# Last feed-forward block: three output tiles preset with x2 in DRAM, their scaled rows from ScalarE added by accumulating transfers

## The chip, the cores and the metric

The kernel runs on one core of a Trainium2 chip. Its time is the device time of one execution in microseconds (us); given is the median of several runs. Beside it stands one execution under the hardware profiler, whose records the pages of this document quote. The engines are TensorE (PE in the profile), VectorE (DVE), ScalarE (ACT), GpSimd (POOL) and SyncE (SP, which only issues transfers).

## What is computed

One layer of a hybrid encoder for a prompt of 2048 rows and 8 x 16 = 128 sample rows, all in float32, 1024 columns wide:

```python
h   = rms_norm(x, g[0]);  z = h @ w_in
att = rms_norm(band_attention(z), g_att);  mem = mlstm(z)
x2  = x + rms_norm(concat(att, mem) @ w_out, g[1])
u   = rms_norm(x2, g[2]) @ w_up             # 2 x 2816 columns
y   = causal_conv3(u) + b_conv
ffn = (gelu(y_gate) * y_up) @ w_down        # 2816 -> 1024
out = x2 + rms_norm(ffn, g[3])              # the output
```

What matters here is the last line: each row of `ffn` is multiplied by `g[3]` and by one factor, 1 / sqrt(mean of its squares + eps), and added to the row of `x2`.

## The kernel before

The 2176 rows are 17 tiles of 128 rows: tiles 0 to 15 are the prompt, tile 16 (`SAMPLE`) the sample rows. After attention and memory, a projection phase writes `x2` tile by tile to DRAM, each tile of 512 KB as its own tensor `x2d[t]` (line 1045). The feed-forward part then runs over three blocks of tiles (`FBLOCKS`); the last one has tiles 12, 13, 14, 15 and SAMPLE, numbered j = 0 to 4.

Each float32 matmul is done as three matmuls on split operands (`mm3`, lines 105 to 107): a high part made by a cast on ScalarE (line 1327, `wdh` for weights, `ah` for activations) and a low part, the difference, made on VectorE (line 1328, `wdl` and `al`). So each load passes through ScalarE, then VectorE, then TensorE. The split buffers rotate: `wdh` and `wdl` have two each, `ah` and `al` share four, and a cast into one waits until TensorE has done with its former contents.

The down projection uses seven products of half blocks (Strassen's scheme, `SEQUENCE`), numbered p = 0 to 6. Each product has three stretches of weights (c = 0 to 2), loaded by `down_rows` (line 1382) from `w_down` or from sums kept in DRAM (`wtd`), and six pieces of activations, loaded by `fetch_a` (lines 1573 and 1576) and split by `split_a`. After each product of the last block, `leave_last` moves or adds the sums from PSUM to the tiles `F_[j]` in SBUF (named `last` in the profile). When half a row (512 columns) is complete, `seal` closes it: ScalarE squares it and sums the squares (line 1705 or 1709), VectorE multiplies it by `g3` (line 1706 or 1708). When both halves are there, GpSimd makes the factor `rs` from the sums (lines 88 and 94), VectorE computes `F * rs + x2` (line 1717) and SP stores the result (line 1718). For j = 0, 1 and 4 this happens after p = 5, while TensorE runs the product p = 6; for j = 2 and 3 after p = 6, at the very end.

The `x2` rows for that sum are loaded at line 1738 into `X_[j]`, tiles that reuse the buffers of the up projection's operands. Tiles of the earlier blocks are finished another way (`later`, lines 1443 to 1452): their scaled rows are added to `x2d` in DRAM by accumulating transfers that GpSimd issues (line 1449), and copied to the output from there (line 1451).

The code is laid out by a framework that orders the instructions of each engine itself, by the order of the code and by when it estimates them ready, and sets all the semaphores. So the order on an engine, and on SP's queue of transfers, need not be that of the code.

Of the kernel before, what the change touches and what calls it, by code (L numbers as in the profile page):

```python
# [12 lines left out]
AF = mybir.ActivationFunctionType  # L13
ALU = mybir.AluOpType
# [26 lines left out]
NK = NF // 2  # L41
FOLD_RATE = 1.0
FAST = (0, 1, 2)
ORDERS = [[f for k in range(NK) for f in (k, k + NK)] if b in FAST else list(range(NF)) for b in range(3)]
B11, B12, B22, B21 = range(4)
T1, T3, T2, T4 = range(4, 8)
# [4 lines left out]
def hymba_step(ctx: ExitStack, tc: tile.TileContext, I: dict, O: dict):  # L51
    nc = tc.nc
# [20 lines left out]
    def dt_(shape, name):  # L73
        return dram.tile(shape, F32, tag=name, name=name)
# [12 lines left out]
    def mean_square(ms, ssq, n, eps=EPS):  # L87
        nc.gpsimd.tensor_scalar(ms, ssq, 1.0 / n, eps, op0=ALU.mult, op1=ALU.add)

    def rsqrt_mean(ssq, n, name, eps=EPS):  # L90
        ms = small.tile([P, 1], F32, tag="ms", name=name + "_ms")
        mean_square(ms, ssq, n, eps)
        rs = small.tile([P, 1], F32, tag="rs", name=name + "_rs")
        nc.gpsimd.tensor_tensor(rs, ms, nhalf[:, 0:1], op=ALU.pow)
        return rs
# [7 lines left out]
    def mm3(out, ah, al, bh, bl, start, stop, onto=False):  # L103
# [18 lines left out]
    f1d = [dt_([P, 512], f"f1d{t}") for t in range(12)]  # L122
    gd = {b: [dt_([P, 768], f"gd{b}_{f}") for f in range(NF)] for b in range(3) if b not in FAST}
    ad = {(b, what): dt_([P, NK, 256 if b == 2 and what in ("A22", "S2", "S3") else 384], f"ad{b}_{what}")
          for b in FAST for what in ("A11", "A12", "A22", "S1", "S2", "S3", "S4")}
    wtd = [dt_([P, 2048], f"wtd{k}") for k in range(NK)]
    wsd = [dt_([P, 2048], f"wsd{f}") for f in range(NF)]
    lated = [dt_([P, 4, 384], f"lated{i}") for i in range(4)]
    x2d = [dt_([P, D], f"x2d{t}") for t in range(17)]
# [1229 lines left out]
    def load_up(b, i, g, quads=None):  # L1359
        f = ORDERS[b][i]  # L1360
        n = 2 * i + g
        nm = f"{b}_{f}_{g}"
        if n % 3 < 2:
            h = wpool.tile([P, 2112], F32R, tag="wh", name=f"wuh{nm}", bufs=2)
            l = wpool.tile([P, 2112], F32R, tag="wl", name=f"wul{nm}", bufs=2)
            at = [(h[:, i * 512:(i + 1) * 512], l[:, i * 512:(i + 1) * 512]) for i in range(4)]
        else:
            t = [p4.tile([P, 1056], F32R, tag="w3", name=f"wu3{nm}_{i}", bufs=4) for i in range(4)]
            at = [tuple(t[2 * x + i // 2][:, i % 2 * 512:i % 2 * 512 + 512] for x in range(2)) for i in range(4)]
        for (h, l), r in zip(at, quads or load_quads(b, f, g)):  # L1370
            split(h, l, r)
        return at
# [46 lines left out]
    def out_rows(t):  # L1419
        return O["y_sample"] if t == SAMPLE else O["y_prompt"][t * P:(t + 1) * P, :]  # L1420
# [63 lines left out]
    for b, tiles in enumerate(FBLOCKS):  # L1484
        last = b == len(FBLOCKS) - 1
        fast = b in FAST
        nt = len(tiles)
# [133 lines left out]
        unfinished = []  # L1621
        for fi, f in enumerate(ORDERS[b]):
            w = pend.pop(0)
# [63 lines left out]
        if fast:  # L1687
# [3 lines left out]
            if last:  # L1691
                place = lambda pool, i: pool.tile([P, 3, D], F32, tag=f"B{i}", name=f"last{i}", bufs=1)
                fa, xa, fb, xb = place(p3, 0), place(p3, 1), place(p4, 3), place(p4, 4)
                F_ = [fa[:, 0], fa[:, 1], fb[:, 0], fb[:, 1], fa[:, 2]]
                X_ = [xa[:, 0], xa[:, 1], xb[:, 0], xb[:, 1], xa[:, 2]]

            def part_of(j, dh):
                return F_[j][:, dh * 512:dh * 512 + 512]

            def seal(j, dh, acc=None):  # L1700

                t, half, gs = tiles[j], part_of(j, dh), g3[:, dh * 512:dh * 512 + 512]
                ssq = p3.tile([P, 1], F32, tag=f"dssq{j}", name=f"dssq{t}_{dh}", bufs=2)
                if acc is None:
                    nc.scalar.activation(junk, half, AF.Square, accum_out=ssq)
                    nc.vector.tensor_tensor(half, half, gs, op=ALU.mult)
                else:
                    nc.vector.tensor_tensor(half, acc, gs, op=ALU.mult)
                    nc.scalar.activation(junk, acc, AF.Square, accum_out=ssq)
                if j not in res:  # L1710
                    mean_square(ssq, ssq, D)
                    res[j] = ssq
                    return
                rs = rsqrt_mean(ssq, D, f"n3_{t}", res[j])
                for c in ((slice(0, D),) if acc is None else (slice(512, D), slice(0, 512))):
                    v = F_[j][:, c]
                    nc.vector.scalar_tensor_tensor(v, v, rs, X_[j][:, c], op0=ALU.mult, op1=ALU.add)
                    nc.sync.dma_start(out_rows(t)[:, c], v)

            def leave_last(p):  # L1720
                acc = sets[SEQUENCE[p][2]]
                for j in range(2):
                    if p == 0:
                        nc.scalar.copy(part_of(j, 0), acc[j])
                    elif p == 2:
                        nc.scalar.copy(part_of(j, 1), acc[j])
                    elif p == 3:
                        nc.scalar.copy(part_of(2 + j, 1), acc[j])
                    elif p == 6:
                        seal(2 + j, 0, acc[j])  # L1730
                    else:
                        x = part_of(*{1: (j, 0), 4: (2 + j, 1), 5: (j, 1)}[p])
                        nc.vector.tensor_tensor(x, x, acc[j], op=ALU.add)
                        seal(*{1: (j, 0), 4: (2 + j, 1), 5: (j, 1)}[p])
                if p == 0:
                    nc.scalar.copy(part_of(4, 1), mms[0])
                    for j in range(5):
                        nc.sync.dma_start(X_[j], x2d[tiles[j]])
                elif p == 1:
                    nc.scalar.copy(part_of(4, 0), mms[0])  # L1740
                    seal(4, 0)
                elif p == 5:
                    nc.vector.tensor_tensor(part_of(4, 1), part_of(4, 1), mms[1], op=ALU.add)
                    seal(4, 1)
# [84 lines left out]
        for dh in range(2):  # L1829
# [57 lines left out]
            for j in order:  # L1887
# [5 lines left out]
                else:  # L1893
# [4 lines left out]
                    rs = p3.tile([P, 1], F32, tag=f"drs{j}", name=f"drs{tiles[j]}", bufs=2)  # L1898
# [101 lines left out]
```

## Time and profile before

| | us |
|---|---|
| median of 3 runs | 2754.65 |
| lowest and highest run | 2751.52, 2759.46 |
| profiled execution, time | 2753.91 |
| profiled execution, span of its records | 2752.2 |

| engine | busy us | share of the span |
|---|---|---|
| TensorE | 2677.0 | 97% |
| VectorE | 1922.8 | 70% |
| ScalarE | 1457.1 | 53% |
| GpSimd | 731.5 | 27% |

The page counts TensorE as busy from a matmul's start to its modelled end. The granted clock, which its other views give, is TensorE's share of full speed. The lines of a timeline read: start, length, engine, line of the kernel, operation, output <- inputs, shapes, count, and in brackets how long the engine stood idle before and what released it. In a view by lines, a group has its count, then busy time in all and the mean of one in nanoseconds, then the idle time ahead of it. A "q" behind an engine's name is its queue of issues.

### The profile page before, as it was taken

Reading aid. Unit: us, or ns where it says so; the run is one execution under the profiler, and the core shown is the slowest. Engines: PE = TensorE matmul, PEld = TensorE weight load, DVE = VectorE, ACT = ScalarE, POOL = GpSimd, SP = SyncE. Lnnn points to the kernel's source line nnn. Section 1 sums busy time; section 2 is a strip of 40 time slices with the busy share of each in tenths; the row PEclk is TensorE's granted clock in tenths of the full one; section 3 lists DMA queues with packets and bytes.
Section 4 is the critical chain, followed back from the end, with each engine's and each line's share of the span. In section 5 each row is a group of like instructions: output and inputs, shape, how many; then the busy total and the mean of one; then the engine's idle time right before and its main releaser. Section 6 shows DMA issues by size and latency. Waiting matters only on the chain.

```text
span 2752.2 us, 47852 instructions
## 1 busy us (share of the span) xinstructions
PE 2677.0 (97%) x16323; PEld 2504.0 (91%) x16323; DVE 1922.8 (70%) x3643; ACT 1457.1 (53%) x2961; POOL 731.5 (27%) x1397
## 2 busy tenths in 40 slices
PE   8999999999999999999999999999999999999998
PEld 7899999998899998878999997799999878999976
DVE  5344456646556667766999997758888866998956
ACT  4355545634356666543555456655455665554554
POOL 1000010211100002344465551123343212556401
PEclk9999999999999999999999999999999999999999
DMA  5534355557564456678776668757886867798875
GB/s 185 159 115 141 104 162 169 165 149 213 155 192 131 139 171 223 195 235 279 286 210 197 198 199 286 239 185 209 240 238 184 263 227 233 228 263 233 252 265 178
DMA packets 337172, 557.04 MB, mean 202 GB/s; under 512 B 62083, under 2 KB 168415, under 8 KB 336799
## 3 DMA queue, kind: packets, MB, share of 16 engines
q1 hardware_dynamic: 252846, 400.31, 47.2%
q0 software_dynamic: 45488, 119.84, 14.8%
q10 hardware_dynamic: 38592, 33.83, 3.7%
q8 instruction: 128, 2.10, 0.3%
q14 instruction: 118, 0.96, 0.1%
HBM read 389.77 MB, written 173.49 MB: 205 GB/s over the span
## 4 chain that ended last, share of the span: by engine, by line
PE 43%; DVE 4%; DMA 3%; issue 1%; ACT 1%; POOL 0%; SPq 0%; DVEq 0%; POOLq 0%; ACTq 0%
PE uec L105 5%; PE uec L106 5%; PE uec L107 5%; PE dn L107 3%; PE dn L105 3%; PE dn L106 3%; PE ua L107 3%; PE ua L106 3%; PE ua L105 3%; PE dnm L107 1%; PE dnm L106 1%; PE ub L107 1%; PE dnm L105 1%; PE ub L105 1%; PE ub L106 1%
## 5 line engine op out<-in xcount | busy, mean ns | idle before, releaser
L105 PE MATMUL uec<-B,wuh 128*128 128x384 f32 (+1 forms) x720 | 236.2, 328 | 6.0 <-DVE ug L1501 3.3
L106 PE MATMUL uec<-B,wuh 128*128 128x384 f32 (+1 forms) x720 | 235.3, 327 | 0.0
L107 PE MATMUL uec<-B,wul 128*128 128x384 f32 (+1 forms) x720 | 234.4, 327 | 0.0
L1327 ACT CAST wuh<-wu 128x512 fp32r<-128x512 f32 x255 | 141.7, 618 | 105.9 <-PE uec L106 104.5
L107 PE MATMUL dn<-wdh,al 128*128 128x512 f32 x462 | 186.0, 403 | 4.7 <-DVE al L1328 4.5
L1328 DVE TENSOR_TENSOR al<-ar,ah 128x768 fp32r<-128x768 f32 (+2 forms) x141 | 108.6, 779 | 116.4 <-ACT ah L1327 114.1
L105 PE MATMUL dn<-wdh,ah 128*128 128x512 f32 x462 | 183.8, 398 | 5.9 <-ACT ah L1327 3.7
L106 PE MATMUL dn<-wdl,ah 128*128 128x512 f32 x462 | 182.6, 395 | 0.0
L1327 ACT CAST ah<-ar 128x768 fp32r<-128x768 f32 (+2 forms) x141 | 96.2, 692 | 152.3 <-PE dnm L106 112.9
L1328 DVE TENSOR_TENSOR wul<-wu,wuh 128x512 fp32r<-128x512 f32 x255 | 164.5, 685 | 2.4 <-ACT wuh L1327 2.4
L406 DVE CUSTOM_DVE_ANT_0 tmp<-s,nb 128x640 f32<-128x640 f32 (+4 forms) x128 | 94.4, 738 | 89.9 <-PE s L396 89.3
L105 PE MATMUL vo<-wi_h,hT 128*128 128x256 f32 x544 | 155.2, 285 | 0.6 <-DVE mt L212 0.6
L107 PE MATMUL vo<-wi_h,hT 128*128 128x256 f32 x544 | 155.6, 286 | 0.0
L106 PE MATMUL vo<-wi_l,hT 128*128 128x256 f32 x544 | 154.8, 285 | 0.0
L1328 DVE TENSOR_TENSOR wdl<-wdr,wdh 128x512 fp32r<-128x512 f32 x231 | 145.5, 686 | 8.5 <-ACT wdh L1327 8.3
L105 PEld LDWEIGHTS uec<-B,wuh 128*128 128x128 f32 x720 | 135.2, 188 | 9.2 <-issue 3.7
L106 PEld LDWEIGHTS uec<-B,wuh 128*128 128x128 f32 x720 | 135.4, 188 | 0.2
L107 PEld LDWEIGHTS uec<-B,wul 128*128 128x128 f32 x720 | 135.1, 188 | 0.0
L105 PE MATMUL qk<-hT,wi_h 128*128 128x384 f32 (+1 forms) x384 | 129.0, 336 | 5.9 <-ACT qk_st L237 5.2
L419 DVE TENSOR_TENSOR ptl<-pt,pth 128x640 fp32r<-128x640 f32 (+4 forms) x128 | 93.6, 738 | 57.8 <-ACT pth L418 56.9
L1327 ACT CAST wdh<-wdr 128x512 fp32r<-128x512 f32 x231 | 127.5, 620 | 11.3 <-PE uec L106 7.5
L407 ACT ACTIVATE tmp<-tmp,mn 128x640 f32<-128x640 f32 (+4 forms) x128 | 97.6, 763 | 64.2 <-DVE mn L406 61.8
(426 smaller groups left out, 9258.8 us busy)
## 6 DMA issues: line engine op xcount, KB each, us to landing
wu<-in_w_up SPq DMA_DIRECT2D x220, 256.0 KB, 4.8
wu<-wsd SPq DMA_DIRECT2D x176, 256.0 KB, 3.4
wdr<-wtd SPq DMA_DIRECT2D x132, 256.0 KB, 4.8
wi_raw<-in_w_in SPq DMA_DIRECT2D x52, 512.0 KB, 4.0
wdr<-in_w_down SPq DMA_DIRECT2D x99, 256.0 KB, 4.7
wsd<-ws POOLq DMA_DIRECT2D x88, 256.0 KB, 4.3
ar<-ad_S SPq DMA_DIRECT2D x50, 384.0 KB, 3.4
kraw<-kTd SPq DMA_DIRECT2D x112, 128.0 KB, 3.3
```

The lines of the kernel that those rows point to most:

```text
L105: nc.tensor.matmul(out, ah, bh, start=start, stop=False, skip_group_check=onto)
L106: nc.tensor.matmul(out, ah, bl, start=False, stop=False, skip_group_check=onto)
L107: nc.tensor.matmul(out, al, bh, start=False, stop=stop, skip_group_check=onto)
L406: nc.vector.tensor_tensor_reduce(o_, s_, b_, 1.0, 3e38, ALU.add, ALU.min, accum_out=mn)
L407: nc.scalar.activation(tmp[:, :n], tmp[:, :n], AF.Exp, bias=mn, scale=-1.0, accum_out=rsum[:, i % 4, hh:hh + 1])
L419: nc.vector.tensor_tensor(s.ptl[:, sl, qc], ptv, s.pth[:, sl, qc], op=ALU.subtract)
L1327: nc.scalar.copy(h, r)
L1328: nc.vector.tensor_tensor(l, r, h, op=ALU.subtract)
```

## The change

For j = 0, 1 and 4 of the last block (tiles 12, 13 and SAMPLE, named `SENT`), `x2` is no longer loaded into SBUF: line 1738 copies it, DRAM to DRAM, into the output rows. When the factor `rs` is known, ScalarE multiplies the 1024 columns of `F_[j]` by it, in place, and GpSimd issues one transfer of 512 KB that adds them to the output rows in DRAM. VectorE's line 1717 and SP's line 1718 remain for tiles 14 and 15 alone.

```diff
+SENT = (0, 1, 4)
...
                 rs = rsqrt_mean(ssq, D, f"n3_{t}", res[j])
+                if acc is None and j in SENT:
+                    nc.scalar.activation(F_[j], F_[j], AF.Copy, scale=rs)
+                    nc.gpsimd.dma_start(out_rows(t), F_[j], accum_op=ALU.add)
+                    return
                 for c in ((slice(0, D),) if acc is None else (slice(512, D), slice(0, 512))):
                     v = F_[j][:, c]
                     nc.vector.scalar_tensor_tensor(v, v, rs, X_[j][:, c], op0=ALU.mult, op1=ALU.add)
...
                     for j in range(5):
-                        nc.sync.dma_start(X_[j], x2d[tiles[j]])
+                        nc.sync.dma_start(out_rows(tiles[j]) if j in SENT else X_[j], x2d[tiles[j]])
```

## The prediction

> **What bounds the kernel now.** I read the page first: the span and the share of each engine.
>
> ```profile
> span 2752.2 us, 47852 instructions
> PE 2677.0 (97%) x16323; PEld 2504.0 (91%) x16323; DVE 1922.8 (70%) x3643; ACT 1457.1 (53%) x2961; POOL 731.5 (27%) x1397
> ```
>
> TensorE (PE) is busy for 97% of the span, so work that moves between other engines counts only where TensorE waits for it. The arithmetic that the change touches (line 1717) runs in the last block, so I read next the chain of work that ended last, in order of time, near the end (start, length, what).
>
> ```profile
> 2734.88 0.60 DVE wdl L1328
> 2735.48 1.20 DVE last L1717
> 2736.68 0.60 DVE wdl L1328
> 2737.28 0.61 DVE al L1328
> 2737.94 0.50 PE dn L107
> ```
>
> Here VectorE (DVE) sets the end, and one of the three instructions that the change removes stands in it. TensorE's timeline shows the price; its third line is the last matmul of the kernel.
>
> ```profile
> 2735.78 0.39 PE L106 MATMUL dn<-wdl,ah 128*128 128x512 f32 x1
> 2737.94 0.50 PE L107 MATMUL dn<-wdh,al 128*128 128x512 f32 x1 [1.77 <-DVE al L1328]
> 2743.07 0.40 PE L107 MATMUL dn<-wdh,al 128*128 128x512 f32 x1
> ```
>
> TensorE stood still for 1.77 us, until `al`, the low part of the activations, came from DVE. The busy times by windows show what followed (columns: length, busy time of PE, PEld, DVE, ACT, POOL, granted clock, DMA share, GB/s).
>
> ```profile
> 2735.55:2738.96 3.41, 1.64 (x7) 1.08 (x6) 2.67 (x4) 0.37 (x1) 0.00 (x0) 0.97 0.77 310
> 2738.96:2742.37 3.41, 3.41 (x9) 2.63 (x9) 0.00 (x0) 0.00 (x0) 0.00 (x0) 0.53 0.00 0
> 2739.00:2742.10 3.10, 3.10 (x8) 2.36 (x8) 0.00 (x0) 0.00 (x0) 0.00 (x0) 0.50 0.00 0
> 2620.00:2625.00 5.00, 3.00 (x12) 1.81 (x12) 1.39 (x2) 1.89 (x4) 0.26 (x1) 1.00 1.08 352
> ```
>
> Right behind a stretch of 3.41 us in which PE worked for 1.64 us, the clock was 0.50 for 3.10 us. That costs another 3.10 x 0.5 = 1.55 us, if the pause caused it. The last row warns that it need not: 2.00 us of idle in five left the clock at 1.00.
>
> **What is removed.** Three additions of 1024 columns leave DVE. Its timeline there, then ScalarE's (ACT):
>
> ```profile
> 2731.19 1.29 DVE L1717 SCALAR_TENSOR_TENSOR last<-last,n_rs,last 128x1024 f32<-128x1024 f32 x1
> 2733.61 1.27 DVE L1717 SCALAR_TENSOR_TENSOR last<-last,n_rs,last 128x1024 f32<-128x1024 f32 x1
> 2735.41 1.27 DVE L1717 SCALAR_TENSOR_TENSOR last<-last,n_rs,last 128x1024 f32<-128x1024 f32 x1
> 2737.20 1.02 DVE L1328 TENSOR_TENSOR al<-ar,ah 128x512 fp32r<-128x512 f32 x2
> ...
> 2729.53 0.62 ACT L1327 CAST ah<-ar 128x512 fp32r<-128x512 f32 x1 [0.58 <-PE dn L106]
> 2730.05 1.66 ACT L1327 CAST wdh<-wdr 128x512 fp32r<-128x512 f32 x3
> 2732.51 0.62 ACT L1327 CAST ah<-ar 128x512 fp32r<-128x512 f32 x1 [0.80 <-PE dn L106]
> 2735.52 0.41 ACT L1327 CAST ah<-ar 128x256 fp32r<-128x256 f32 x1 [2.38 <-DVE wdl L1328]
> ```
>
> From 2731.19 DVE worked without a pause, and each addition held its queue for 1.2 us, 3.6 us in all. The late `al` needs only the `ah` that ACT finished at 2732.51 + 0.62 = 2733.13. Without the additions DVE gets to it at 2737.20 - 3.6 = 2733.6 and is done at 2734.2. PE wants it when the matmul of 2735.78 lets it go on, at 2737.94 - 1.77 = 2736.17. So the pause has a slack of about 2 us and goes, if ACT keeps its times. Next late would be the third `wdl`, which moves to about 2733 and is early too; then nothing but PE's own matmuls.
>
> **What ACT gets.** Three scalings of 1024 columns by a per-row factor. No such instruction is in the trace; the nearest:
>
> ```profile
> L229 ACT ACTIVATE hT<-xr 128x1024 fp32r<-128x1024 f32 x17 | 18.0, 1058 | 11.2 <-DMA xr<-in_x_prompt 7.7 <-DMA xr<-in_x_sample 3.3
> L1520 ACT ACTIVATE y<-uu,wcv 128x768 f32<-128x768 f32 x44 | 45.3, 1030 | 52.0 <-DVE uu L1663 52.0
> L1524 ACT ACTIVATE y<-y 128x768 f32<-128x768 f32 x44 | 37.3, 847 | 79.9 <-DVE y L1522 79.9
> ```
>
> 1024 columns take 1.06 us without a factor per row; a factor and an offset per row add 1.03 - 0.85 = 0.18 us. Each scaling lies between 1.06 and 1.24; I take 1.15, so 3.45 us for three. ACT's own gaps before 2735.52 are 0.80 + 2.38 = 3.18 us, and each factor comes from GpSimd (POOL):
>
> ```profile
> 2728.40 0.89 POOL L94 TENSOR_TENSOR n_rs<-n_ms,nhalf 128x1 f32<-128x1 f32 x1
> 2731.49 1.39 POOL L94 TENSOR_TENSOR n_rs<-n_ms,nhalf 128x1 f32<-128x1 f32 x1
> 2745.02 0.27 POOL L88 TENSOR_SCALAR n_ms<-dssq,dssq 128x1 f32<-128x1 f32 x1 [12.13 <-ACT junk L1709]
> ```
>
> The first factor is ready at 2729.3, the third at 2732.9. Behind a waiting scaling on ACT's queue stand the casts that make `wdh` and `ah`, and behind those DVE and PE. If all three scalings go ahead of the `ah` of 2732.51, it ends at 2729.53 + 0.6 + 1.6 + 3.45 + 0.6 = 2735.8, `al` follows at 2736.5, and PE waits 0.3 us beyond the 2736.17. If one goes behind it, nothing waits. I keep 0.3 us.
>
> **The transfers.** Three stores of SP's queue (line 1718) become accumulating transfers issued by POOL. Before, nothing of the remaining weight loads stood behind those stores. On POOL an issue takes 0.89 us (first row below), 2.7 us in all, inside the 12.13 us in which POOL waited; if two issues go ahead of the third factor, that one is 1.8 us later.
>
> ```profile
> L1449 POOL DMA_DIRECT2D x2d<-f x24: 842/894/3290, 1896.2 to 2524.7; - x24
> ...
> DMA to landing us min/median/max: 4.7/6.4/9.0
> ...
> 2746.74 2.86 SPq L1718 DMA_DIRECT2D out_y_prompt<-last  x4
> ```
>
> The existing accumulating transfers of 256 KB land after 4.7 to 9.0 us. For 512 KB I bound the time by 4.7 below and twice 9.0 = 18 above, and take twice 4.7 = 9.4, since the queues are nearly empty there (DMA share 0.00 in the rows from 2739 on). The last scaling ends near 2735.5, its issue at 2736.4, and its data land near 2745.8, ahead of the four last stores, which SP issues from 2746.74 on. So I cost them at nothing; at 18 us the last would land at 2754.4 and would itself be the end. The Trainium skill, "DMA: Bandwidth & Descriptors", section "Anatomy of one DMA — SWDGE (gpsimd) path", gives about 2.0 us plus bytes over 436 GB/s; as an estimate that is 3.2 us here, and the sum would be the same.
>
> **The presets.** Three of the five loads of x2 (line 1738) become copies from x2 to the output, both in DRAM: the same bytes read, the same count of issues, but no buffer to wait for. Where do they go? SP's queue is not in code order, as the second row shows: line 1905, the program's second last transfer, stands among weight loads at 2607. The others show the loads now, and when x2 is stored and lands, and how SP has waited for such landings from 1200 to 1400 us (total, times, longest).
>
> ```profile
> L1738 SPq DMA_DIRECT2D last<-x2d x5: 319/422/524, 2585.8 to 2593.4; - x5
> 2607.17 0.42 SPq L1905 DMA_DIRECT2D out_conv_prompt<-halo  x1
> L1045 SPq DMA_DIRECT2D x2d<-mx x17: 319/326/446, 1072.8 to 1327.1; - x17
> DMA to landing us min/median/max: 2.6/4.7/9.3
> SPq L1018 <- DMA x2d<-mx: 31.2, 8, 9.0
> ...
> 1200.00:1330.00 130.00, 125.81 (x604) 101.98 (x603) 84.03 (x114) 53.98 (x110) 65.66 (x114) 1.00 0.89 301
> 2610.00:2640.00 30.00, 26.73 (x114) 20.79 (x113) 16.48 (x26) 13.65 (x24) 4.50 (x7) 1.00 0.91 315
> ```
>
> A preset may therefore stand anywhere after its x2 has landed, more than a thousand us early. Wherever PE has cover it costs nothing, which is my central value. The bounds: at worst each of the three blocks SP for 4.7 us in front of other loads, 14.1 us, and their 1.57 MB take 5.2 us at the 301 GB/s of that window, whose DMA share is already 0.89: 19.3 us. At best the 1.57 MB that are missing from 2585 to 2593 shorten the 3.27 us that PE idles from 2610 to 2640.
>
> **Sum.** -1.77 (pause) - 1.55 (half clock) + 0.3 (ACT) + 0 (transfers, presets) = -3.0 us. The profiled execution took 2753.91 us, 1.7 more than its span, and would become 2750.9. The median of the runs, 2754.65, is 0.74 above it, so I forecast 2751.6 us. The work after the last matmul, 2752.2 - 2743.5 = 8.7 us, stays. That is 0.11% less, under the 0.3% (8.3 us) which a measurement of this kernel can about tell from no change.
>
> **Rivals.**
> 1. The half clock stays. For it: the idle of 2620 to 2625 left the clock at 1.00, so 1.77 us need not be what lowered it. Against: the row of 1.64 us busy in 3.41 stands just ahead of the half clock. Then only 1.77 - 0.3 = 1.5 us go: 2753.2 us. The Trainium skill, "TensorE: Matmul & The Clock Gate", section "Part 1: The HAM clock gate", speaks for this rival: it has the clock fall after at least one idle window of about 3.4 us, which PE did not have here; the length of the slow stretch agrees with its window.
> 2. Presets early and in the way (slower than before). They stand behind the stores of x2 between about 1200 and 1330 us and hold up SP's loads, with the DMA share at 0.89. It decides once they cost PE more than the 3.0 us gained. For it: SP waited up to 9.0 us for just such landings; against: PE was 97% busy there all the same, so loads have some cover. Half of its bound is 9.6 us: 2761 us, at the bound 2771.
> 3. Faster than the sum: the loads from 2585 on have the queues to themselves, and the 3.27 us after 2610 go as well: 2748.3 us. A changed order of SP's queue could also remove other waits, which I cannot price; against it: those loads were issued by 2593.4, 17 us before that stretch begins.
> 4. ACT or the accumulation late. The third factor waits behind two POOL issues (1.8 us) and its scaling stands ahead of `ah`: the pause returns at 0.3 + 1.8 = 2.1 us, and nothing is gained: 2755 us. Or the last accumulation lands at 2754.4 and the time is 2757.
>
> **How the numbers follow.** The forecast has 0.37, rival 1 0.12, rival 2 0.30, rival 3 0.13 and rival 4 0.08. Faster by over 0.3% (below 2746.4) needs rival 3 and more: 0.12, with a part of the forecast's spread. Slower by over 0.3% (above 2762.9) needs the upper half of rival 2 and some of its neighbours: 0.22. The rest, 0.66, is within. The range leaves out the upper end of rival 2 and the unpriced part of rival 3: 2744 to 2764.
>
> **What would show it.** Right: no line 1717 of 1024 columns on DVE; PE's pause before the last 16 matmuls below 0.5 us; clock 1.00 to the last matmul, near 2740; three ACT scalings of about 1.15 us between 2729 and 2736; accumulations landed by 2746. Wrong: a half clock without a pause; SP waiting for x2 to land at more places from 1200 to 1330 us, with PE idle above 4.2 us there; the chain ending in a POOL transfer.

## The result and the profile after

The changed kernel took 2763.12 us, the median of 11 runs (2758.05 to 2770.87); the kernel before, in the same sitting, 2755.06 us (11 runs, 2751.30 to 2763.36). The ratio is 1.0025, with an interval from 1.0013 to 1.0037: by this ratio the change costs some 7 us, where 3 us less was forecast. A second set of runs of the same kernel gave 1.0018 [1.0006, 1.0029]. Both intervals leave 1.0 out, and both central values lie under the 0.3% called measurable in the prediction. One execution of a kernel further down (presets late) took 3731.02 us at a mean granted clock of 0.655, and ratios leave it out.

The profiled execution of the changed kernel was the longest of its 11 runs (2770.87 us), so its times can't be subtracted from those of before as they stand. I read it stage by stage instead. First the page, then the three scalings by lines (durations in ns: least, median, most), and TensorE's timeline at the end, each of the changed kernel:

```profile
span 2769.2 us, 47845 instructions
PE 2682.8 (97%) x16323; PEld 2508.4 (91%) x16323; DVE 1919.7 (69%) x3640; ACT 1460.2 (53%) x2964; POOL 729.8 (26%) x1400
...
L1717 ACT ACTIVATE last<-last,n_rs x3: 1136/1140/1147, 2751.1 to 2753.2; 128x1024 f32<-128x1024 f32 x3
...
2755.27 0.39 PE L107 MATMUL dn<-wdl,ah 128*128 128x512 f32 x1
2755.66 0.50 PE L108 MATMUL dn<-wdh,al 128*128 128x512 f32 x1
2759.23 0.40 PE L108 MATMUL dn<-wdh,al 128*128 128x512 f32 x1
```

Three instructions went from VectorE to ScalarE (3643 to 3640, 2961 to 2964). Between the `wdl,ah` and the `wdh,al` matmul, where TensorE stood still for 1.77 us before, the second starts at 2755.66, when the first ends. GpSimd's last issue, the busy times by windows with the clock, the transfers there (size, us from issue to landing) and the last issues of SP:

```profile
2754.67 0.85 POOL L1718 DMA_DIRECT2D out_y_sample<-last  x1 [0.17 <-issue]
...
2751.00:2754.40 3.40, 3.40 (x17) 2.77 (x16) 2.21 (x4) 3.40 (x5) 3.00 (x4) 1.00 0.32 19
2754.40:2757.80 3.40, 3.39 (x14) 2.25 (x13) 1.03 (x2) 0.81 (x2) 0.95 (x2) 1.00 0.90 163
2757.80:2761.20 3.40, 1.83 (x8) 1.13 (x7) 0.77 (x2) 0.69 (x2) 0.00 (x1) 1.00 1.03 199
...
out_y_prompt<-last POOLq DMA_DIRECT2D x2, 512.0 KB, 7.0
out_y_sample<-last POOLq DMA_DIRECT2D x1, 512.0 KB, 9.9
...
2762.91 2.94 SPq L1723 DMA_DIRECT2D out_y_prompt<-last  x4
```

The clock is 1.00 to the last matmul. So the end of the kernel went as forecast: from the 16300th matmul to the last one this execution takes 3.12 us less than before. One thing there was not forecast: from the end of the last matmul (2759.23 + 0.40) to the end of the span it takes 9.5 us, where before it was 8.7.

The loss must lie elsewhere. The presets (line 1743 now) went where rival 2 of the prediction had put them, more than a thousand us early:

```profile
L1743 SPq DMA_DIRECT2D out_y_prompt<-x2d x2: 553/559/565, 1304.3 to 1319.5; - x2
L1743 SPq DMA_DIRECT2D out_y_sample<-x2d x1: 737/737/737, 1235.0 to 1235.0; - x1
```

But SP did not wait longer for landings of `x2` because of them. These are the rows of its waits, in the first and the second profile of the changed kernel (us in total, times, longest):

```profile
SPq L1019 <- DMA x2d<-mx: 33.4, 8, 8.6
...
SPq L1019 <- DMA x2d<-mx: 34.9, 8, 8.5
```

Before it was 31.2 us, 8 times, and in a kernel without early copies (presets in the middle, below) 33.4 us, 8 times. What TensorE waited for between 1300 and 1380 us had changed, though. Its waits in the second profile of the changed kernel:

```profile
PE ua L106 <- ACT mt L1035: 1.8, 1, 1.8
PE wo L108 <- DVE mt L213: 0.9, 1, 0.9
PE uec L106 <- ACT wu L1328: 0.9, 1, 0.9
PE ub L108 <- DVE wu L1329: 0.6, 1, 0.6
```

A product of the up projection (`ua`) now waits for ScalarE's reading of the projection phase's last sums (`mt`). That set the question for the runs.

### Which instructions moved

The traces also give the order in which the instructions stand on each engine. Between before and after, 423 of TensorE's 16323 matmuls and some 240 instructions of VectorE stand elsewhere in the order, and about 110 each of ScalarE and GpSimd; SP's queue has the three copies put in and is otherwise the same up to the last block. Apart from the end and from single records, the differences belong to the stretch from about 1320 to 1535 us: the change from the projection phase to the first up projection. The framework, which lays out each engine's instructions by its estimates, put work of the up projection in another order there: on TensorE the products of `ua` with `wu` come ahead of those with `wul`, and VectorE's additions of `fold` no longer stand in a row. I call this the new order. In the runs below, "the order of before" means that TensorE's matmuls stand in the same order as before from the first to the last, and VectorE's instructions too, but for one near 1239 us and the three that the change removes. Why a copy of 512 KB makes the framework choose it, its estimates would say; that is not among what the runs show.

### The profile page after: what moved, and what is told of

It reads as the page before. It is cut to its first block, busy times and chain, and to the rows that moved or that the text cites. A ratio compares the mean times of both kernels' runs of the same rounds, so it can differ in the third digit from the quotient of the medians.

```text
span 2769.2 us, 47845 instructions
## 1 busy us (share of the span) xinstructions
PE 2682.8 (97%) x16323; PEld 2508.4 (91%) x16323; DVE 1919.7 (69%) x3640; ACT 1460.2 (53%) x2964; POOL 729.8 (26%) x1400
```

## The experiments

**The theories.** A: the early copies take time from other transfers (bytes, or blocking in SP's queue). B: the copies cost little, and the new order of the other engines' instructions costs. C: the end of the kernel costs (ScalarE, or accumulating transfers). The first runs take the parts of the change one at a time. The expectations of the first four runs use the letters otherwise: their A is that early presets cost, for whatever reason, their B that the end costs, which is C here. The later ones call A here "bytes" and B here "order".

**Presets alone, early.** The copies are made at the changed kernel's place, and the end is that of before.

```diff
                     for j in range(5):
+                        if j in SENT:
+                            nc.sync.dma_start(out_rows(tiles[j]), x2d[tiles[j]])
                         nc.sync.dma_start(X_[j], x2d[tiles[j]])
```

> The kernel before, plus the three DRAM-to-DRAM presets, which stand at the same three places of SP's queue as in the changed kernel (about 1235, 1304 and 1320 us); x2 is still loaded and VectorE still adds it, so the last stores write over the presets. Theory A (the presets standing early cost about 10 us between 1235 us and the end, the last block saves 3.3): 2765 us, about +10 on before, with a ratio near 1.0036. Theory B (the presets are free, the accumulating transfers or the ScalarE scalings cost 7 us): 2755 us, ratio 1.000. In the trace A expects the matmuls from 1400 us on to be 5 us or more later than in the kernel before, measured from those at 1200 us.

Measured: 2763.74 us against 2752.34, ratio 1.0036 [1.0022, 1.0050]. So the loss comes with the early copies, not with the end (C falls). This kernel has the new order.

**Presets in the middle.** They are held in the code's order in the second block of the feed-forward part, so they start far behind the crowded stretch; the end is that of the changed kernel.

```diff
+            if b == 1 and fi in (8, 10, 12):
+                t_ = FBLOCKS[2][SENT[(fi - 8) // 2]]
+                tc.keep_in_program_order(nc.sync.dma_start(out_rows(t_), x2d[t_]))
...
-                        nc.sync.dma_start(out_rows(tiles[j]) if j in SENT else X_[j], x2d[tiles[j]])
+                        if j not in SENT:
+                            nc.sync.dma_start(X_[j], x2d[tiles[j]])
```

> The change with its presets moved: they are pinned in the code of the second feed-forward block (its 9th, 11th and 13th column group, about 1900 to 1950 us), where TensorE was busy without a pause. ScalarE scalings and accumulating transfers as in the change; the order of instructions on TensorE is that of the kernel before. Theory A: the 3.3 us of the last block stay and nothing else changes, 2751.8 us, ratio 0.9988. Theory B: as the changed kernel, 2762 us. In the trace both expect the last pause of TensorE and the half clock to be gone.

Measured: 2750.56 us, 0.9996 [0.9987, 1.0005]. The loss is gone. This kernel has the order of before up to the last block. Its gain is not measurable.

**Presets late.** They are held at the place where the code has them, ahead of the last product.

```diff
-                        nc.sync.dma_start(out_rows(tiles[j]) if j in SENT else X_[j], x2d[tiles[j]])
+                        if j in SENT:
+                            tc.keep_in_program_order(nc.sync.dma_start(out_rows(tiles[j]), x2d[tiles[j]]))
+                        else:
+                            nc.sync.dma_start(X_[j], x2d[tiles[j]])
```

> The change with its presets pinned behind the weight loads of the first product of the last block (about 2590 to 2640 us), where the DMA engines are 0.9 to 1.0 busy. Theory A: no cost at 1300 us; the 1.57 MB fall into the full queues instead, so between 2752 (hidden) and 2757 us (1.57 MB at 301 GB/s are 5.2 us, all of it in front of loads that TensorE waits for). Theory B: as the changed kernel, 2762 us.

Measured: 2752.30 us, 0.9996 [0.9985, 1.0008]; the order of before. The copies have a place where they cost nothing measurable at either end of the feed-forward part.

**No presets, plain stores.** GpSimd's transfers store instead of adding.

```diff
-                    nc.gpsimd.dma_start(out_rows(t), F_[j], accum_op=ALU.add)
+                    nc.gpsimd.dma_start(out_rows(t), F_[j])
...
-                        nc.sync.dma_start(out_rows(tiles[j]) if j in SENT else X_[j], x2d[tiles[j]])
+                        if j not in SENT:
+                            nc.sync.dma_start(X_[j], x2d[tiles[j]])
```

> The last block's part alone: ScalarE scales the three tiles and GpSimd stores them with an ordinary transfer; there are no presets and no x2 is added to these three tiles, a part of the computation that is left out. Theory A: 2751.8 us as with the presets in the second block, ratio 0.9988. Theory B, if the accumulation is what costs: 2751.8 as well; if the scalings or GpSimd's issues cost: 2762 us.

In this kernel `x2` is not added to the three tiles. Measured: 2753.26 us, 1.0004 [0.9992, 1.0016]. Even without copies and without adding in DRAM nothing measurable is gained. Accumulation itself is not what the change pays for.

So far early copies and the new order came together. The next runs part them: which of the copies brings the order, and does the loss follow the bytes or the order?

**Two of three early (tile 12 and SAMPLE).** Tile 13's copy is held in the middle.

```diff
+            if b == 1 and fi in (8, 10, 12)[:1]:
+                t_ = FBLOCKS[2][(1,)[(fi - 8) // 2]]
+                tc.keep_in_program_order(nc.sync.dma_start(out_rows(t_), x2d[t_]))
...
-                        nc.sync.dma_start(out_rows(tiles[j]) if j in SENT else X_[j], x2d[tiles[j]])
+                        if j in (0, 4):
+                            nc.sync.dma_start(out_rows(tiles[j]), x2d[tiles[j]])
+                        elif j not in SENT:
+                            nc.sync.dma_start(X_[j], x2d[tiles[j]])
```

> The change with two of its three presets early, where they stood (SAMPLE near 1235, tile 12 near 1304 us); the third, tile 13, is pinned in the second block near 1900 us. So 1.05 of the 1.57 MB are early, but the order of instructions on TensorE, VectorE, ScalarE and GpSimd is that of the kernel before up to the last block. Theory bytes (the early 1.57 MB in the full DMA queues are what costs): two thirds of the cost remain, the stretch from 1223 to 1375 us is 3 us longer than before, time 2757 us. Theory order (the third preset makes the framework lay out the start of the feed-forward part in another order, and that order is worse): 0 us in that stretch, time as with all presets in the second block, 2750.6 us.

Measured: 2753.14 us against 2752.01, 1.0001 [0.9988, 1.0013], with the order of before. Two thirds of the early bytes cost nothing measurable. The stretch from 1223 to 1375 us is 2.26 us longer all the same, where the theory of the order expected 0 and that of the bytes 3; the stages below come back to it.

**One of three early (tile 13).** The other two are held in the middle.

```diff
+            if b == 1 and fi in (8, 10, 12)[:2]:
+                t_ = FBLOCKS[2][(0, 4)[(fi - 8) // 2]]
+                tc.keep_in_program_order(nc.sync.dma_start(out_rows(t_), x2d[t_]))
...
-                        nc.sync.dma_start(out_rows(tiles[j]) if j in SENT else X_[j], x2d[tiles[j]])
+                        if j in (1,):
+                            nc.sync.dma_start(out_rows(tiles[j]), x2d[tiles[j]])
+                        elif j not in SENT:
+                            nc.sync.dma_start(X_[j], x2d[tiles[j]])
```

> The change with only the third preset early (tile 13, between 1308 and 1320 us), the other two pinned in the second block. The order of instructions is that of the changed kernel, with a third of the early bytes. Theory bytes: 1.6 us longer from 1223 to 1375 us, time 2753 to 2754 us. Theory order: the whole cost, 4.7 us in that stretch, time 2760 us or more.

Measured: 2754.42 us, 1.0012 [1.0001, 1.0022], with the new order. It is tile 13's copy that brings the order. Half the bytes of the run above cost more by the central values; the two intervals overlap. The time is nearer to what the theory of the bytes expected (2753 to 2754) than to the 2760 of the order; the stretch from 1223 to 1375 us, 4.16 us longer, is nearer to the 4.7 of the order than to 1.6.

**Tile 13 a little later.** Its copy is held 13 issues further on in SP's queue, where it started at 1344 us; the other two stay in the middle.

```diff
+            if (b, fi) in ((0, 1), (1, 8), (1, 10)):
+                t_ = {1: 13, 8: 12, 10: SAMPLE}[fi]
+                tc.keep_in_program_order(nc.sync.dma_start(out_rows(t_), x2d[t_]))
...
-                        nc.sync.dma_start(out_rows(tiles[j]) if j in SENT else X_[j], x2d[tiles[j]])
+                        if j not in SENT:
+                            nc.sync.dma_start(X_[j], x2d[tiles[j]])
```

> As the kernel with only tile 13's preset early, but that preset is pinned thirteen issues further on in SP's queue, behind the first loads of the feed-forward weights (about 1330 us); the others are in the second block. The same bytes in the same full queues, but the order of instructions of the kernel before. Theory bytes: 1.6 us or more from 1223 to 1375 us (this transfer stands right among the loads that TensorE waits for), time 2753 us. Theory order: under 1 us there, time 2751 us.

Measured: 2751.54 us, 0.9995 [0.9984, 1.0006], with the order of before. The same 512 KB, some 32 us later counted from the same matmul, cost nothing measurable. The stretch from 1223 to 1375 us is 2.14 us longer, though, where the theory of the order expected under 1 and that of the bytes 1.6 or more.

**A copy of 64 KB.** As the run before last, but of tile 13 only the first 16 rows are preset early; `x2` is not added to its other 112 rows.

```diff
-                            nc.sync.dma_start(out_rows(tiles[j]), x2d[tiles[j]])
+                            nc.sync.dma_start(out_rows(tiles[j])[0:16, :], x2d[tiles[j]][0:16, :])
```

> Only tile 13's preset early, and of it only 16 of the 128 rows (64 KB), so x2 is not added to the other 112 rows of that tile, a part of the computation that is left out; the other two presets are in the second block. The framework lays out the start of the feed-forward part in a third order, other than that of the kernel before and that of the change. Theory bytes: nothing, 2750.6 us, 0 us from 1223 to 1375 us. Theory order: some cost of its own, of a size that cannot be told beforehand, 2 to 8 us.

Measured: 2757.45 us, 1.0017 [1.0005, 1.0030]. I had meant this as the copy without its bytes. The framework answered with a third order (on TensorE 845 matmuls stand elsewhere than before, 569 elsewhere than after), so it doesn't hold the order fixed. What it does show: with an eighth of one tile's bytes the loss is there.

Then the test in which all bytes are early and only the order is that of before, and beside it three repeats.

**All three early, in the order of before.** Tile 12 and SAMPLE are free, tile 13 is held as in the run "a little later".

```diff
+            if b == 0 and fi == 1:
+                tc.keep_in_program_order(nc.sync.dma_start(out_rows(13), x2d[13]))
...
-                        nc.sync.dma_start(out_rows(tiles[j]) if j in SENT else X_[j], x2d[tiles[j]])
+                        if j in (0, 4):
+                            nc.sync.dma_start(out_rows(tiles[j]), x2d[tiles[j]])
+                        elif j not in SENT:
+                            nc.sync.dma_start(X_[j], x2d[tiles[j]])
```

> The change with all three presets early, but with the order of instructions of the kernel before up to the last block: SAMPLE and tile 12 where they stood in the change, tile 13 pinned thirteen issues further on in SP's queue (about 1330 us). So the same 1.57 MB of early copies as in the change; only the order differs. Theory bytes: as the changed kernel, near 2760 us, ratio 1.0025. Theory order: the bytes cost what they cost by twos and ones, about 2 us each time from 1223 to 1375 us, so at most 4 us there, of which the following stretch gives some back, 2752 to 2755 us, ratio 0.9995 to 1.0010.

Measured: 2751.62 us against 2753.32, 0.9994 [0.9985, 1.0003].

**Repeats** of the changed kernel, of the presets in the middle, and of the kernel before, each unedited.

> The changed kernel once more, for a second profile and beside the others on one chip. Theory order: again 4 to 5 us longer from 1223 to 1375 us, and no wait of 4.9 us at 2415 to 2437 us, if that one was chance; if it is the order's, it comes again. Ratio near 1.0025.

> The change with its three presets in the second block once more. If the half clock at the end is part of every execution of the kernel before, 3.1 us less than before, ratio 0.9989; if only of some, between 1.6 and 3.1 us less, ratio 0.9989 to 0.9994.

> The kernel before once more, for a second profile and as the measure of what the comparison itself makes of no difference: ratio 1.000. In its profile the pause of 1.77 us ahead of the last matmuls must come again; whether the half clock behind it does is open.

Measured: 2757.05 us, 1.0018 [1.0006, 1.0029]; 2752.76 us, 0.9996 [0.9983, 1.0009]; 2750.77 us, 0.9996 [0.9985, 1.0008]. The changed kernel and the kernel with all copies early do the same work with the same transfers. Their intervals don't overlap, and they are 5.4 us apart. The presets in the middle were expected at 0.9989 to 0.9994 and came out a little above. No version beats the kernel before by what these runs can tell: its own repeat also came out at 0.9996.

The profiles of these two show where. Both rows of tile 13's copy on SP's queue first (27 us apart), then two windows of each, then TensorE's waits from 1300 to 1380 us. The changed kernel, second profile (its waits stand above):

```profile
1311.09 0.55 SPq L1743 DMA_DIRECT2D out_y_prompt<-x2d  x1
1320.00:1330.00 10.00, 8.21 (x34) 7.30 (x33) 7.16 (x11) 4.44 (x7) 3.70 (x6) 0.83 1.01 412
1330.00:1340.00 10.00, 8.49 (x47) 7.85 (x47) 10.00 (x13) 6.54 (x8) 2.58 (x5) 1.00 1.00 401
...
1324.91 0.45 PE L106 MATMUL ua<-B,wu 128*128 128x384 f32 x1 [1.79 <-ACT mt L1035]
```

All early, in the order of before:

```profile
1337.98 0.56 SPq L1629 DMA_DIRECT2D out_y_prompt<-x2d  x1
1320.00:1330.00 10.00, 9.48 (x54) 8.89 (x52) 10.00 (x15) 8.93 (x13) 4.99 (x9) 1.00 1.01 405
1330.00:1340.00 10.00, 8.82 (x50) 8.38 (x50) 10.00 (x13) 3.85 (x6) 1.42 (x3) 1.00 0.95 334
...
PE ua L108 <- DVE wul L1329: 0.9, 2, 0.5
PE uec L106 <- DVE x L1645: 0.7, 1, 0.7
PE wo L108 <- DVE mt L213: 0.4, 1, 0.4
```

In 1320 to 1330 the transfers are as dense in both (DMA share 1.01, 412 and 405 GB/s), so it is not the bandwidth in that window that differs. The engines do less: VectorE is busy for 7.16 us instead of 10.00, TensorE works on 34 matmuls instead of 54. But VectorE's missing 2.84 us are the end of one wait, and that wait is for a transfer. The first row is of the changed kernel, second profile, the second of all early; each is followed by the time to landing of the two loads of `w_down` (`fold`, issued by GpSimd near 1312 and 1311 us) that it waited for:

```profile
1322.84 0.69 DVE L1188 TENSOR_TENSOR fold<-fold,fold 128x512 f32<-128x512 f32 x1 [5.64 <-DMA fold<-in_w_down]
DMA to landing us min/median/max: 10.6/11.0/11.5
...
1318.20 2.15 DVE L1188 TENSOR_TENSOR fold<-fold,fold 128x512 f32<-128x512 f32 x3 [2.58 <-DMA fold<-in_w_down]
DMA to landing us min/median/max: 7.7/7.9/8.0
```

In both, `mx` stands behind this addition on VectorE, ScalarE's `mt` waits for `mx`, and TensorE's `ua` goes on within 0.2 us of the end of `mt` (1324.77 and 1321.58). In the changed kernel the two loads are issued right behind tile 13's copy (1312.12 and 1312.65 against 1311.09). So the wait of 1.8 us for `mt` need not be the order's. The waits for `wu` (`uec`, 0.9 us, and `ub`, 0.6) stand in all four profiles of the new order and in none with the order of before.

TensorE waits 1.8 + 0.9 + 0.9 + 0.6 = 4.2 us against 0.9 + 0.7 + 0.4 = 2.0 us, which is 2.2 us more. And the mean clock is 0.83 over 10 us: a stretch of 3.4 us at 0.50, which costs 1.7 us. Together 3.9 us, and between 1223 and 1375 us the two profiles differ by 4.1 us (4.16 - 0.05 in the table below).

### Where the time went, by stages

Executions of one kernel differ by some us, and most of that arises ahead of the change. So I took the time between the same matmuls of each trace, counted from the first: the 8250th (1223 us in the first profile of before), the 9000th (1375), the 11250th (1815), the 16300th (2734) and the last (2743). The table has the time of each stretch less that of the first profile of before; the last column is the time from the end of the last matmul to the end of the span, as it stands.

| profile | order | early copies, MB | 1223 to 1375 | 1375 to 1815 | both | 2734 to last | behind last |
|---|---|---|---|---|---|---|---|
| before | before | 0 | 0 | 0 | 0 | 0 | 8.7 |
| before, again | before | 0 | +2.87 | -3.09 | -0.22 | -1.57 | 8.7 |
| mid | before | 0 | +0.70 | -2.00 | -1.30 | -3.13 | 9.5 |
| mid, again | before | 0 | -0.04 | -3.76 | -3.80 | -3.12 | 9.5 |
| late | before | 0 | +0.37 | -4.75 | -4.38 | -3.12 | 8.9 |
| plain stores | before | 0 | -0.18 | -3.16 | -3.34 | -3.14 | 9.1 |
| tile 13 a little later | before | 0.52 | +2.14 | -2.77 | -0.63 | -3.12 | 9.1 |
| tile 12 and SAMPLE early | before | 1.05 | +2.26 | -1.89 | +0.37 | -3.12 | 9.6 |
| all early | before | 1.57 | +0.05 | +0.39 | +0.44 | -3.11 | 9.5 |
| tile 13 early | new | 0.52 | +4.16 | +0.12 | +4.28 | -3.14 | 8.9 |
| presets alone | new | 1.57 | +4.72 | -0.34 | +4.38 | -1.56 | 9.0 |
| after | new | 1.57 | +4.87 | +0.54 | +5.41 | -3.12 | 9.5 |
| after, again | new | 1.57 | +4.16 | -0.60 | +3.56 | -3.11 | 9.6 |
| 64 KB of tile 13 early | third | 0.07 | +3.39 | +4.25 | +7.64 | -3.14 | 8.9 |

In the column "both" the four profiles of the new order lie between +3.56 and +5.41, mean +4.4. The three with early copies in the order of before lie between -0.63 and +0.44, mean +0.06. The two groups don't touch, and within each the bytes make no difference: 0.52 MB cost as much as 1.57. So **the order costs about 4.4 us**, as far as it can be parted from the late loads shown above, which come next. The six without early copies have a mean of -2.2 us, with a spread from -4.38 to 0. That the copies as such cost the 2.2 us between is possible, but the times of these kernels (0.9994 to 1.0001 with early copies, 0.9996 to 1.0004 without) don't show it. It stays open.

The late loads can be followed through the profiles. VectorE waited for those two loads for 2.6 to 3.2 us in six of the nine profiles with the order of before, and there the first stretch has -0.18 to +0.70. It waited 4.0, 4.1 and 5.0 us in the other three (tile 12 and SAMPLE early, tile 13 a little later, before again), and there the first stretch has +2.26, +2.14 and +2.87. The last of these has no early copy at all (and a half clock of 1.7 us in the 2.87). So in the order of before a late landing goes with 2 to 3 us in that stretch, with or without early copies, and this fits the two expectations that were missed above. In the new order the wait was 4.8 to 6.1 us; some 2 of the 4.2 to 4.9 us there may be the landing's. It does not account for the column "both": the three with the order of before stand at -0.63 to +0.37 there, and tile 13 early, whose first load landed no later than theirs (98.2 us behind the 8250th matmul, against 98.3 to 98.5), at +4.28. In the 64 KB run VectorE waited 3.0 us, and its third order stands at +7.64. So theory B holds for the larger part. No run has the new order without a full copy just ahead of those loads, and what costs TensorE its time behind 1375 us was not taken apart.

A half clock of 3.4 us between 1323 and 1343 us stands in all four profiles of the new order and in that of the third, and in one of the nine of the order of before (before again, where TensorE had just waited 2.5 us). It is part of the 4.4 us; that TensorE's waits there bring it on is argued from the place alone. These rows are of presets alone and of mid:

```profile
1330.00:1340.00 10.00, 7.36 (x30) 6.72 (x31) 10.00 (x13) 4.20 (x6) 1.78 (x4) 0.83 0.88 347
```

```profile
1330.00:1340.00 10.00, 8.82 (x49) 8.12 (x48) 10.00 (x13) 4.68 (x6) 0.73 (x2) 1.00 0.92 352
```

The balance, with the second profile of before as the usual one: 4.4 us for the order, 2.2 that may be the copies', -1.6 for the end and up to +0.9 behind the last matmul. That is +2.8 to +5.9 us. Measured were 1.0018 and 1.0025, which is 5.0 and 6.9 us, with lower bounds of 1.7 and 3.6. For presets alone, with the end of before, the balance is 4.4 to 6.6 us, where 1.0036 is 9.9 us with a lower bound of 6.1; it has the fewest runs (5), the profiled one is the shortest of them, and some 3 us stay unexplained.

## Why the prediction was wrong

**The step that failed** is the term for the presets: "Wherever PE has cover it costs nothing, which is my central value." The prediction asked whether TensorE had cover for the transfers, and it largely had: all three copies early, in the order of before, cost nothing measurable. It did not ask what else the framework would lay out anew around a copy that is ready a thousand us early, though it said that SP's queue is not in code order, and named a changed order of that queue only as a possible gain. The instructions of the other engines changed their order as well, in a stretch of some 200 us that holds none of the lines of the diff but the copies, and that is where the time went: +4.4 us where 0 stood in the sum, of which some 2 may be the late landing of two loads behind tile 13's copy. The bounds of 0 and 19.3 us held it.

**Rival 2** (2761 us, 0.30) was right in place and sign, and near in size. Its mechanism, copies that hold up SP's loads, is not what happened: SP's waits for `x2` went from 31.2 to 33.4 and 34.9 us, in as many waits (33.4 without early copies too), and all three copies early, in the order of before, cost nothing measurable. Its test, "SP waiting for x2 to land at more places", came out negative while the time came out on its side. What did land later behind tile 13's copy are two loads of GpSimd's, as shown above; the rival named SP's loads alone.

**The pause** (-1.77 us) was right. It stands in the second profile of before and in that of presets alone, where the additions are still on VectorE, and in no profile with ScalarE's scalings. Before, again, and presets alone:

```profile
2734.71 0.50 PE L107 MATMUL dn<-wdh,al 128*128 128x512 f32 x1 [1.77 <-DVE al L1328]
2734.00:2737.40 3.40, 2.69 (x12) 2.22 (x13) 0.99 (x3) 0.00 (x0) 0.00 (x0) 1.00 0.39 157
```

```profile
2742.00 0.50 PE L108 MATMUL dn<-wdh,al 128*128 128x512 f32 x1 [1.77 <-DVE al L1329]
```

**The half clock** (-1.55 us) was a term mis-sized. The first row above is the same pause, to the hundredth, and the window around it has the clock at 1.00. Of three profiles with the pause one has the half clock behind it. No profile without the pause has one there, which fits the pause as its cause but does not show it with a single case; it belongs to some executions: the end is worth 3.1 us against the first profile of before and 1.6 us against the other, and a median holds between them. Rival 1 was right for two profiles in three. Its page, the Trainium skill, "TensorE: Matmul & The Clock Gate", section "Part 1: The HAM clock gate", lets its window of about 3.4 us run free of what the kernel does; that would fit a pause which now falls within one window and now across two. The trace does not agree with the page's one idle window or more: a window of 3.41 us that still held 1.64 us of work stood ahead of the half clock.

**ScalarE** (1.15 us each, +0.3 us in all): measured 1.14 us each, and no pause came back: right, and the 0.3 us is not to be seen.

**The accumulating transfers** (9.4 us, hidden): they landed after 7.0 us in the median of two and 9.9 us, as taken. They are not quite hidden. Behind the last matmul 8.7 us were to stay; it is 8.9 to 9.6 us with accumulating transfers, 9.0 with the presets alone, 9.1 with plain stores. The last of them was issued at 2754.67 and landed 9.9 us later, at 2764.6, when the four last stores, issued from 2762.91 on, were on their way. That these are slowed by that rest is argued from the place alone; no run took it apart, and it is at most 0.9 us.

**Faster by the load queue** (rival 3): the three loads that left line 1738 gave nothing that could be told: the kernel with the presets in the middle has three loads fewer there and a ratio of 0.9996.

Two things in the first profile of the changed kernel are chance: 8.0 us more ahead of the 8250th matmul, and 4.9 us between 2437 and 2448 us. Neither is in the second profile.

## What to carry to other kernels

A transfer that becomes free of a buffer becomes free in time as well: under a framework that orders instructions itself, ask where its earliest place is, hold it in the code's order where it is wanted, and compare the order of all the engines before and after, not only of the queue that it is on. When a small change costs more than its parts, part "the bytes" from "the order" with two kernels that do the same work and differ only in the place of one instruction; here a copy 27 us later was worth 5.4 us. And a term read from one profiled execution, such as a half clock, is worth its share over several profiles, not its whole size.

## What was not expected of the hardware

Accumulating transfers into DRAM fill the DMA engines at half the rate of ordinary ones: shares of 0.90 and 1.03 at 163 and 199 GB/s in the last windows of the changed kernel, where ordinary traffic at 1.00 to 1.01 moves 401 to 412 GB/s. Three such transfers of 512 KB kept the engines busy for more than 6 us and landed after 5.5, 8.5 and 9.9 us. In the kernel with plain stores, the same three transfers at the same place moved 377 GB/s at a share of 0.96 and landed after 3.0, 3.5 and 3.8 us:

```profile
2730.00:2733.40 3.40, 3.40 (x15) 2.24 (x14) 1.03 (x2) 0.98 (x3) 0.53 (x1) 1.00 0.96 377
DMA to landing us min/median/max: 3.0/3.5/3.8
```

The clock falls in some executions and not in others for the same pause of 1.77 us at the same matmul: 0.50 for 3.10 us in one profile, 1.00 in another.
